# One chain for all sixteen causal heads, with the next head's logits ahead of the value product

## The chip, the cores and the metric

The kernel runs on one core of one Trainium2 chip. The metric is device microseconds (us) of one execution, and the median of several runs is what counts. The engines are TensorE (PE, with its weight loads PEld), VectorE (DVE), ScalarE (ACT), GpSimd (POOL) and SyncE (SP), whose queue issues the transfers.

## The reference

Two layers, each a SwiGLU half step, a mixing block and a second SwiGLU half step, on 512 tokens of width 1024. The mixing block has three branches on the same normalised input. Cut to the two causal branches:

```python
def block(args):                      # stick-breaking: 8 heads of 64
    z = q k^T * scale
    mask = key_pos < q_pos
    log_beta = log_sigmoid(z)
    log_not = where(mask, log_beta - z, 0)
    log_between = cumsum(log_not, reverse) - log_not
    w = where(mask, exp(log_beta + log_between), 0)
    return w @ v

def block(args):                      # forgetting: 8 heads of 64
    z = q k^T * scale + c_q - c_k     # c = cumsum(log_sigmoid(f))
    p = softmax(where(key_pos <= q_pos, z, min))
    return p @ v
...
merged = g_sb * (o_sb @ w_br_sb) + g_fx * (o_fx @ w_br_fox) + g_mem * (o_mem @ w_br_mem)
h = h + rmsnorm(merged @ w_out)       # g_* = sigmoid(u @ w_gate + b_gate)
```

The third branch is attention over 256 memory rows with four heads of 128.

## The kernel before

Every float32 matrix is kept as a high part and a low part, and a product is three matmuls (lines 210 to 212, `mm3`), each over 512 columns as a rule. The weights come as float32 from HBM in units of 512 KB (`raw_...`, a ring of two buffers), are split by ACT (high part, `wh_...`) and DVE (low part, `wl_...`) into rings of four, and are consumed once. On PE the matmuls therefore stand close behind each other almost everywhere, as long as weights and PSUM banks are there.

The order on PE is written by a planner at build time, `Queue`. It holds a list of jobs: the projections of q, k and v (`pq`, `pk`, `pv`), the gates (`pg`: input by `w_gate`, then a sigmoid) and the branch products (`pb`: attention output by `w_br`, times the gate). Beside the jobs runs a *chain*, a generator of the attention heads. `weave` goes on with the chain when its due time is reached, and fills the time until then with jobs, each counted by its columns (`PE_US`). A chain yields `("pe", t)` for work of its own on PE and `("wait", t)` for the time of other work that it asks for before its next stage. Jobs past a `limit` may not be taken yet; if no job is left, the planner's clock only jumps, and the next stage of the chain stands right behind the last on PE. `Q.past(n, t, limit)` runs the jobs up to number n and then up to `t` us of the job after it. A scheduler still places instructions of ACT, DVE and POOL among each other; the matmuls of a value product are pinned.

A causal head has four stages with three waits between them:

- Logits (`zs` for stick-breaking, line 1198; `zf` for forgetting, lines 1241 to 1252) and what ACT and DVE make of them: sigmoids and a product scan (lines 1204 to 1211), or maximum, exponential and division (1254 to 1258). Then a wait of `W_SB0` or `W_FX0`.
- The weights, float32, are taken apart into planes of 16 bits by ACT (`turn_out`, line 1137) and transposed by three transfers on SP's queue (`turn_over`, line 1146). Then `W_SB1` or `W_FX1`.
- The planes are joined again (`joined`, line 1156, by ACT for `pws`, by DVE for `pwf`) and split into high and low parts `pts`, `ptf` (lines 180 and 181). Then `W_SB2` or `W_FX2`.
- The value product (`attend`, line 1170, eight matmuls into `pvs` or `pvf`), and the head's output o (lines 1173 to 1175).

Before, the eight stick-breaking heads are woven one by one: a head's logits stand behind the value product of the head before. The eight forgetting heads are already one chain, `foxes`, in which the next head's logits are issued where a head asks for its last wait, `W_FX2`. Head names are layerless pairs: `1_0` is pair 1, head 0; the forgetting pairs go in the order 2, 3, 0, 1, so `1_1` is the last head of a layer.

Gates are computed in two ways (`sigmoid_neg`, lines 196 to 206): while `direct` is set, during the stick-breaking heads, by one ACT instruction (line 199); afterwards, with ACT's exponential and logarithm table, by four of ACT and one of DVE (lines 202 to 206). `forget_cumsum` (lines 1338 to 1349) needs the exponential and logarithm in the middle of the stick-breaking heads and changes tables there and back. The gate's PSUM bank comes free with DVE's instruction of line 205 or ACT's of line 199. There are four banks for jobs and value products together (`mm`) and four for logits (`z`).

Of the kernel before, what the change touches and what calls it, by code (L numbers as in the profile page):

```python
# [23 lines left out]
def kernel(  # L24
# [46 lines left out]
    NP = 4  # L71
# [30 lines left out]
    def stile(shape, tag, name, dt=F32R):  # L102
        return sb.tile(shape, dt, tag=tag, bufs=BUFS[tag], name=name)

    def blk(tag, name):
        return stile([P, 2, S], tag, name)
# [86 lines left out]
    def functions(name):  # L193
        tc.keep_in_program_order(nc.scalar.preload_act_table_set(name))
# [273 lines left out]
    Q = Queue()  # L468
# [710 lines left out]
    def cuts(name):  # L1179

        t = stile([P, CUT], "rs", "cut" + name, F32)
        nc.gpsimd.memset(t[:], 0.0)
        for c, before in ((CUT - 2 * P, 1), (CUT - P, 0)):
            o = t[:, c - before:c + P]
            nc.gpsimd.affine_select(out=o, in_=o, pattern=[[-1, P + before]], compare_op=ALU.not_equal, fill=1.0,
                                    base=before - 1, channel_multiplier=1)
        return t

    def stick_head(q, k, vts, pj, j, cut, ot, name):

        groups = []
        for rows in ((3,), (2,), (1, 0)):
            pz = pbank("z", f"z{name}_{rows[0]}")
            w0 = (rows[0] + 1) * P
            for i in rows:
                o = pz[:, (rows[0] - i) * 2 * P:][:, :max((i + 1) * P, 2 * P)]
                for kk in (j, 2 + j):
                    nc.tensor.matmul(o, q[:, j, i * P:(i + 1) * P], k[:, kk, :o.shape[1]], start=(i == rows[0] and kk == j),
                                     stop=(kk == 2 + j), skip_group_check=True)
            w = w0 + (len(rows) - 1) * P  # L1200
            zr, t, n = pz[:, :w], tmp(f"t{name}_{rows[0]}"), tmp(f"n{name}_{rows[0]}")

            nc.gpsimd.memset(t[:, w - 1:w], 0.0)
            nc.scalar.activation(n[:, :w], zr, AF.Sigmoid, scale=-1.0)
            nc.scalar.activation(t[:, :w - 1], zr[:, :w - 1], AF.Sigmoid)
            if len(rows) > 1:
                nc.vector.memset(n[:, w0:w0 + 1], 0.0)
            c1 = CUT if len(rows) > 1 else CUT - P
            back, one = n[:, 1:w][:, ::-1], cut[:, c1 - w:c1 - 1][:, ::-1]
            nc.vector.tensor_tensor_scan(back, back, one, 0.0, ALU.mult, ALU.add)  # L1210
            nc.vector.tensor_tensor(t[:, :w - 1], t[:, :w - 1], n[:, 1:w], ALU.mult)
            groups.append((rows, w, t, n))
        yield ("pe", 1.4)
        yield ("wait", W_SB0)
        for _, w, t, n in groups:
            turn_out(t, w, n)
            turn_over(n, w, t)
        yield ("wait", W_SB1)
        tri = joined([(rows, w, t) for rows, w, t, _ in groups], nc.scalar.copy, name)
        yield ("wait", W_SB2)  # L1220
        attend(pbank("mm", "pv" + name), j, vts, pj, tri, ot, name)
        yield ("pe", 1.2)

    def fox_pre(q, k, j, hd, cs, name):

        r, ro, _ = HEAD_ROWS[j]
        rs_ = slice(ro.start, min(ro.stop, 104))
        qk = stile([P, 2, S], "rs", "qk" + name)
        nc.gpsimd.tensor_copy(qk[r, 0], q[r, j])
        nc.gpsimd.tensor_copy(qk[r, 1], k[r, 2])  # L1230
        nc.gpsimd.memset(qk[ro, 0].bitcast(F32), 1.0)
        nc.vector.tensor_scalar(qk[rs_, 1], cs[rs_].bitcast(F32), sel[rs_, hd:hd + 1], None, ALU.mult)
        return qk
# [84 lines left out]
        split(ot[:, 0], ot[:, 1], pv[:])  # L1318
        yield ("pe", 1.3)

    W_SB0, W_SB1, W_SB2 = 7.0, 7.0, 5.0
    W_FX0, W_FX1, W_FX2 = 2.0, 6.3, 5.0
    W_MM0, W_MM1 = 6.0, 6.0
    W_K = 4.0

    FOX = (2, 3, 0, 1)
# [28 lines left out]
    def mixing(l, src, ks, vs, rest, dst):  # L1355
# [5 lines left out]
        st, marks = {}, {}  # L1361
# [138 lines left out]
        heads, fox = [(0, p) for p in range(NP)] + [(1, p) for p in FOX], []  # L1500
# [20 lines left out]
        limits = [marks["before", *h] for h in heads[2:]] + 3 * [marks["gates", 1]]  # L1521
        limits = [[min(n, marks["gates", 0]) if i < NP else n for n in limits[i:i + 2]] for i in range(len(heads))]
# [10 lines left out]
        def run():  # L1533
            Q.until(marks["first"])
            for i in range(NT):
                nc.sync.dma_start(hsave[i], hT[i][:])
            st["o", 2] = [blk("o", f"om{l}_{i}") for i in range(NMH)]

            def mems():
                def head(i):  # L1540
                    Q.until(marks["qm", i // 2])
                    return mem_head(st["qm"][i], ks, vs, i, st["o", 2][i], f"m{l}_{i}",
                                    lambda: Q.until(marks["values"]))


                def part(g):
                    for kind, us_ in g:
                        yield (kind, us_)
                        if kind == "wait":
                            return  # L1550
                gen = head(0)
                yield from part(gen)
                for i in range(NMH):
                    if i + 1 < NMH:
                        following = head(i + 1)
                        yield from ((k_, u_) for k_, u_ in part(following) if k_ == "pe")
                    for kind, us_ in gen:
                        if kind == "wait" and i + 1 == NMH:

                            Q.past(marks[0, 0], W_K, marks[0, 1])  # L1560
                            functions("sigmoid_and_others")
                            st["direct"] = True
                            begun[0, 0] = stick(0, 0)
                            yield next(begun[0, 0])
                        yield kind, us_
                    gen = following

            def stick(p, j):
                return stick_head(st["q", 0, p], st["k", 0, p], st["v", 0, p // 2], p % 2, j, st["cut"], st["o", 0][p],
                                  f"s{l}_{p}_{j}")  # L1570

            def pre(at, j):

                if j == 2:
                    at, j = at + 1, 0
                p = FOX[at] if at < NP else None
                if (p, j) not in fx and ("k", 1, p) in st:
                    fx[p, j] = fox_pre(st["q", 1, p], st["k", 1, p], j, 2 * p + j, st["cs"], f"{l}_{p}_{j}")

            def fox(at, j):  # L1580
                pre(at, j)
                p = FOX[at]
                return fox_head(st["q", 1, p], st["k", 1, p], st["v", 1, p // 2], p % 2, j, fx[p, j], st["o", 1][p],
                                f"f{l}_{p}_{j}", lambda: pre(at, j + 1))

            begun, fx = {}, {}
            st["cut"] = cuts(f"{l}")
            st["o", 0] = [blk("o", f"o{l}_0_{p}") for p in range(NP)]
            Q.weave(mems(), marks[0, 1])
            for p in range(NP):  # L1590
                Q.past(marks[0, p], W_K, limits[p][0])
                for j in range(2):
                    Q.weave(begun.pop((p, j), None) or stick(p, j), limits[p][j])
            functions("natural_log_exp_and_others")
            st["direct"] = False
            st["o", 1] = [blk("o", f"o{l}_1_{p}") for p in range(NP)]
            order = [(at, j) for at in range(NP) for j in range(2)]
            now = [0]

            def foxes():  # L1600

                def head(n):
                    at, j = order[n]
                    Q.past(marks[1, FOX[at]], W_K, limits[NP + at][0])
                    return fox(at, j)
                gen = head(0)
                for n in range(len(order)):
                    for kind, us_ in gen:
                        if us_ is W_FX2:
                            if n + 1 < len(order):  # L1610
                                following = head(n + 1)
                                yield next(following)
                            now[0] = min(n + 1, len(order) - 1)
                        yield kind, us_
                    gen = following

            def limit():
                at, j = order[now[0]]
                return limits[NP + at][j]
            Q.weave(foxes(), limit)  # L1620
            Q.until(limits[-1][-1])

        marks["run"] = run
# [110 lines left out]
    for l in LAYERS:  # L1734
        i, mn = 3 * l, []
# [43 lines left out]
```

## Time and profile before

| | |
|---|---|
| median of three runs | 2362.8 us (2358.9 to 2363.26) |
| the profiled execution | 2357.57 us, span from the first to the last instruction 2355.8 us |
| PE busy | 2310.8 us, 98% of the span |
| PEld, DVE, ACT | 1947.8 us (83%), 1795.6 us (76%), 1546.7 us (66%) |
| mean granted TensorE clock | 0.993 |
| layer 0: first stick-breaking logits to last forgetting value product | 434 to 782 us |
| layer 1: the same | 1602 to 1950 us |

Times in the views count from the span's start. A bracket behind an instruction is the idle time of its engine just before it, and what ended that idle time. Matmuls overlap: one over 512 columns is listed with 0.39 us, and the next starts 0.23 us after it.

### The profile page before, as it was taken

How to read it: one execution, taken by the hardware profiler on the slowest of the kernel's cores; microseconds unless marked ns; L12 is line 12 of the kernel's file. 1: busy time of each engine (PE TensorE's matmuls, PEld its weight loads, DVE VectorE, ACT ScalarE, POOL GpSimd, SP SyncE). 2: the span in 40 equal slices, each digit the busy share in tenths (PEclk: the TensorE clock that was granted, in tenths of full speed). 3: DMA queues.
4: the chain of work that ended last, by engine and by line, in shares of the span. 5: the costliest groups of instructions: out<-in, count | busy, mean ns of one | idle time of the engine just before them, and what ended most of it. 6: DMA issues, size and time to landing. Idle time of an engine off the chain costs nothing.

```text
span 2355.8 us, 30462 instructions
## 1 busy us (share of the span) xinstructions
PE 2310.8 (98%) x11303; PEld 1947.8 (83%) x11303; DVE 1795.6 (76%) x2285; ACT 1546.7 (66%) x2232; POOL 88.8 (4%) x182
## 2 busy tenths in 40 slices
PE   9999999999999899999999999999999989999998
PEld 8888888988887698888898888888888867888887
DVE  8877876656787688878798787765667876888785
ACT  6676565677778456774656765646787784567744
POOL 0000000001111000000000000000001200000000
PEclk9999999999999999999999999999999999999999
DMA  6667454354544655674646655533355455566744
GB/s 206 198 179 214 145 198 131 83 128 99 132 114 117 206 188 160 196 189 156 229 143 188 204 164 193 180 107 103 104 123 127 101 150 188 170 184 181 221 137 143
DMA packets 382841, 375.93 MB, mean 160 GB/s; under 512 B 163274, under 2 KB 274146, under 8 KB 382692
## 3 DMA queue, kind: packets, MB, share of 16 engines
q1 hardware_dynamic: 382596, 373.95, 54.3%
q8 instruction: 89, 1.46, 0.3%
q14 instruction: 60, 0.49, 0.1%
q0 software_dynamic: 96, 0.03, 0.0%
HBM read 319.39 MB, written 16.78 MB: 143 GB/s over the span
## 4 chain that ended last, share of the span: by engine, by line
PE 82%; DVE 6%; DMA 5%; ACT 5%; issue 2%; DVEq 0%; SPq 0%; ACTq 0%
PE pda L211 3%; PE pda L210 3%; PE pda L212 3%; PE pg L210 2%; PE pg L211 2%; PE pg L212 2%; PE pdc L211 2%; PE pdc L212 2%; PE pdc L210 2%; DMA pf<-nf 2%; PE pb L210 2%; PE pb L211 2%; PE pb L212 1%; PE pwc0g L210 1%; PE pwc1g L211 1%
## 5 line engine op out<-in xcount | busy, mean ns | idle before, releaser
L210 PE MATMUL pg<-us_a,wh_wg 128*128 128x512 f32 x384 | 150.1, 391 | 1.3 <-DVE k L181 1.3
L211 PE MATMUL pg<-us_a,wh_wg 128*128 128x512 f32 x384 | 149.6, 389 | 0.0
L212 PE MATMUL pg<-us_a,wl_wg 128*128 128x512 f32 x384 | 149.5, 389 | 0.0
L181 DVE TENSOR_TENSOR wl_da<-raw_da,wh_da 128x1024 fp32r<-128x1024 f32 x50 | 60.8, 1223 | 45.9 <-ACT wh_da L180 45.9
L181 DVE TENSOR_TENSOR wl_dc<-raw_dc,wh_dc 128x1024 fp32r<-128x1024 f32 x50 | 61.0, 1223 | 43.4 <-ACT wh_dc L180 43.4
L211 PE MATMUL pdc<-wl_dc,ahc 128*128 128x512 f32 x224 | 87.6, 391 | 0.0
L211 PE MATMUL pda<-wl_da,aha 128*128 128x512 f32 x224 | 87.6, 391 | 0.0
L212 PE MATMUL pda<-wh_da,ala 128*128 128x512 f32 x224 | 87.2, 389 | 0.0
L212 PE MATMUL pdc<-wh_dc,alc 128*128 128x512 f32 x224 | 87.2, 389 | 0.0
L210 PE MATMUL pdc<-wh_dc,ahc 128*128 128x512 f32 x224 | 86.5, 389 | 0.0
L210 PE MATMUL pda<-wh_da,aha 128*128 128x512 f32 x224 | 86.5, 389 | 0.0
L210 PEld LDWEIGHTS pg<-us_a,wh_wg 128*128 128x128 f32 x384 | 72.4, 188 | 16.7 <-PE pb L212 2.0
L212 PEld LDWEIGHTS pg<-us_a,wl_wg 128*128 128x128 f32 x384 | 72.1, 188 | 15.3
L211 PEld LDWEIGHTS pg<-us_a,wh_wg 128*128 128x128 f32 x384 | 72.3, 188 | 14.6
L180 ACT CAST wh_dc<-raw_dc 128x1024 fp32r<-128x1024 f32 x50 | 52.3, 1050 | 47.5 <-DMA raw_dc<-in_ffn_w_down_dram 16.1
L180 ACT CAST wh_da<-raw_da 128x1024 fp32r<-128x1024 f32 x50 | 52.1, 1049 | 46.8 <-PE pda L212 14.1
L184 DVE SCALAR_TENSOR_TENSOR wl_wg<-raw_wg,wh_wg 128x1024 fp32r<-128x1024 f32 x48 | 59.3, 1239 | 29.6 <-ACT wh_wg L183 29.3
L180 ACT CAST wh_uc<-raw_uc 128x1024 fp32r<-128x1024 f32 x44 | 46.4, 1054 | 38.0 <-PE pwc1g L212 9.2
L180 ACT CAST wh_ua<-raw_ua 128x1024 fp32r<-128x1024 f32 x44 | 46.2, 1053 | 32.9 <-PE pwa1g L212 9.3
L181 DVE TENSOR_TENSOR wl_uc<-raw_uc,wh_uc 128x1024 fp32r<-128x1024 f32 x44 | 53.7, 1220 | 16.7 <-ACT wh_uc L180 16.7
L183 ACT ACTIVATE wh_wg<-raw_wg 128x1024 fp32r<-128x1024 f32 x48 | 50.6, 1058 | 19.3 <-PE pv L1123 7.7
L181 DVE TENSOR_TENSOR wl_ga<-raw_ga,wh_ga 128x1024 fp32r<-128x1024 f32 x40 | 48.4, 1219 | 18.7 <-ACT wh_ga L180 18.7
(643 smaller groups left out, 7984.8 us busy)
## 6 DMA issues: line engine op xcount, KB each, us to landing
raw_da<-in_ffn_w_down_dram SPq DMA_DIRECT2D x66, 512.0 KB, 4.9
raw_dc<-in_ffn_w_down_dram SPq DMA_DIRECT2D x66, 512.0 KB, 4.6
raw_ga<-in_ffn_w_gate_dram SPq DMA_DIRECT2D x52, 512.0 KB, 4.7
raw_ua<-in_ffn_w_up_dram SPq DMA_DIRECT2D x52, 512.0 KB, 4.5
raw_gc<-in_ffn_w_gate_dram SPq DMA_DIRECT2D x52, 512.0 KB, 4.2
raw_uc<-in_ffn_w_up_dram SPq DMA_DIRECT2D x52, 512.0 KB, 4.4
raw_wg<-in_w_gate_dram SPq DMA_DIRECT2D x48, 512.0 KB, 3.5
raw_wo<-in_w_out_dram SPq DMA_DIRECT2D x24, 512.0 KB, 3.8
```

What stands on the lines that cost most here:

```text
L180: both = [nc.scalar.copy(h_ap, src)]
L181: make = lambda: nc.vector.tensor_tensor(l_ap, src, h_ap.bitcast(F32), ALU.subtract)
L183: both = [nc.scalar.activation(h_ap, src, AF.Copy, scale=scale)]
L184: make = lambda: nc.vector.scalar_tensor_tensor(l_ap, src, scale, h_ap.bitcast(F32), ALU.mult, ALU.subtract)
L210: nc.tensor.matmul(pt, lh, rh, start=start, stop=False, skip_group_check=free)
L211: nc.tensor.matmul(pt, lh, rl, start=False, stop=False, skip_group_check=free)
L212: nc.tensor.matmul(pt, ll, rh, start=False, stop=stop, skip_group_check=free)
```

## The change

The sixteen causal heads of a layer, eight stick-breaking and then eight forgetting, become one chain, `causal`. In all of them the next head's first stage, its logits, is issued where a head has joined its planes and asks for its last wait. The first forgetting head's logits so stand ahead of the last stick-breaking head's value product, and the change of ACT's tables to exponential and logarithm, with `direct` cleared, comes with them. The waits are set anew: the sum of a stick-breaking head's three goes from 19.0 to 16.1, that of a forgetting head from 13.3 to 13.2. `Q.past` is called only ahead of the first head of a pair, and the limit on jobs is that of the head whose logits were issued last.

```diff
-    W_SB0, W_SB1, W_SB2 = 7.0, 7.0, 5.0
-    W_FX0, W_FX1, W_FX2 = 2.0, 6.3, 5.0
+    W_SB0, W_SB1, W_SB2 = 5.0, 6.0, 5.1
+    W_FX0, W_FX1, W_FX2 = 2.0, 6.0, 5.2
...
-            Q.weave(mems(), marks[0, 1])
-            for p in range(NP):
-                Q.past(marks[0, p], W_K, limits[p][0])
-                for j in range(2):
-                    Q.weave(begun.pop((p, j), None) or stick(p, j), limits[p][j])
-            functions("natural_log_exp_and_others")
-            st["direct"] = False
-            st["o", 1] = [blk("o", f"o{l}_1_{p}") for p in range(NP)]
-            order = [(at, j) for at in range(NP) for j in range(2)]
+            order = [(br, i, j) for br in range(2) for i in range(NP) for j in range(2)]
             now = [0]
...
+            def head(n):
+                br, i, j = order[n]
+                if (br, i, j) == (1, 0, 0):
+                    functions("natural_log_exp_and_others")
+                    st["direct"] = False
+                    st["o", 1] = [blk("o", f"o{l}_1_{p}") for p in range(NP)]
+                if j == 0 and n:
+                    Q.past(marks[heads[br * NP + i]], W_K, limit())
+                return (fox if br else stick)(i, j)
...
+            def causal(gen):
                 for n in range(len(order)):
                     for kind, us_ in gen:
-                        if us_ is W_FX2:
+                        if kind == "wait" and us_ in (W_SB2, W_FX2):
                             if n + 1 < len(order):
                                 following = head(n + 1)
                                 yield next(following)
-                            now[0] = min(n + 1, len(order) - 1)
+                                now[0] = n + 1
                         yield kind, us_
                     gen = following
...
+            Q.weave(mems(), marks[0, 1])
+            Q.weave(causal(begun[0, 0]), limit)
             Q.until(limits[-1][-1])
```

The numbers of matmuls, vector instructions and transfers stay what they were, but for the gates: 28 instead of 22 take the longer way in the two layers together (18 more ACT instructions, 6 of DVE), and ACT's table loads go from 17 to 21.

How the program's order moves is shown at three places. First PE in layer 0, between the stick-breaking heads 1_0 and 1_1; `pvs_1_0` is the value product of the first, `zs_1_1` are the logits of the second, and L210 to L212 are matmuls of jobs. Before:

```order
L212 MATMUL pg_1_1_4519<-us_a_0_2946,wl_wg_1_0_0_4261 128x512
L1170 MATMUL pvs_1_0_4526<-pts_1_0_4493,v_0_0_1_3771 128x256 x4
L1170 MATMUL pvs_1_0_4526<-pts_1_0_4493,v_0_0_0_3695 128x384 x2
L1170 MATMUL pvs_1_0_4526<-pts_1_0_4493,v_0_0_0_3695 128x512 x2
L1198 MATMUL zs_1_1_3_4540<-k_0_1_3924,q_0_1_3882 128x512 x2
L1198 MATMUL zs_1_1_2_4550<-k_0_1_3924,q_0_1_3882 128x384 x2
L1198 MATMUL zs_1_1_1_4560<-k_0_1_3924,q_0_1_3882 128x256 x4
L210 MATMUL pg_1_1_4519<-us_a_0_2946,wh_wg_1_0_0_4260 128x512
```

And now:

```order
L212 MATMUL pg_2_3_4421<-us_a_0_2946,wl_wg_2_1_0_4089 128x512
L1198 MATMUL zs_1_1_3_4439<-k_0_1_3924,q_0_1_3882 128x512 x2
L1198 MATMUL zs_1_1_2_4449<-k_0_1_3924,q_0_1_3882 128x384 x2
L1198 MATMUL zs_1_1_1_4459<-k_0_1_3924,q_0_1_3882 128x256 x4
L210 MATMUL pg_2_3_4421<-us_a_0_2946,wh_wg_2_1_0_4088 128x512
...
L212 MATMUL pb_2_3_4492<-om_1_3329,wl_wb_2_1_0_4101 128x512
L1170 MATMUL pvs_1_0_4499<-pts_1_0_4434,v_0_0_1_3771 128x256 x4
L1170 MATMUL pvs_1_0_4499<-pts_1_0_4434,v_0_0_0_3695 128x384 x2
L1170 MATMUL pvs_1_0_4499<-pts_1_0_4434,v_0_0_0_3695 128x512 x2
L210 MATMUL pb_2_3_4492<-om_2_3330,wh_wb_2_1_0_4100 128x512
```

The logits have moved ahead of the value product, with 24 matmuls of jobs in between; from this value product to the next there are 90 matmuls of jobs before and 78 now (54 up to the next logits, 24 behind them).

Second, PE in layer 0 at the last two forgetting heads, 1_0 and 1_1, whose value products are `pvf_1_0` and `pvf_1_1`. Before:

```order
L212 MATMUL pg_1_6_6887<-us_a_1_2947,wl_wg_1_3_4_6546 128x512
L1170 MATMUL pvf_1_0_6912<-ptf_1_0_6824,v_1_0_1_5807 128x256 x4
L1170 MATMUL pvf_1_0_6912<-ptf_1_0_6824,v_1_0_0_5705 128x384 x2
L1170 MATMUL pvf_1_0_6912<-ptf_1_0_6824,v_1_0_0_5705 128x512 x2
L210 MATMUL pg_1_7_6933<-us_a_0_2946,wh_wg_1_3_0_6539 128x512
...
L212 MATMUL pg_1_7_6933<-us_a_1_2947,wl_wg_1_3_4_6546 128x512
L1170 MATMUL pvf_1_1_6985<-ptf_1_1_6980,v_1_0_1_5807 128x256
L210 MATMUL pb_1_0_7027<-o_1_0_5577,wh_wb_1_0_0_6721 128x512
```

And now:

```order
L212 MATMUL pb_0_7_6796<-o_0_1_3341,wl_wb_0_3_0_6410 128x512
L1170 MATMUL pvf_1_0_6803<-ptf_1_0_6725,v_1_0_1_5925 128x256 x4
L1170 MATMUL pvf_1_0_6803<-ptf_1_0_6725,v_1_0_0_5845 128x384 x2
L1170 MATMUL pvf_1_0_6803<-ptf_1_0_6725,v_1_0_0_5845 128x512 x2
L210 MATMUL pb_0_7_6796<-o_0_2_3342,wh_wb_0_3_0_6409 128x512
...
L212 MATMUL pg_1_6_6933<-us_a_1_2947,wl_wg_1_3_4_6650 128x512
L1170 MATMUL pvf_1_1_6949<-ptf_1_1_6897,v_1_0_1_5925 128x256 x4
L1170 MATMUL pvf_1_1_6949<-ptf_1_1_6897,v_1_0_0_5845 128x384 x2
L1170 MATMUL pvf_1_1_6949<-ptf_1_1_6897,v_1_0_0_5845 128x512 x2
```

Between the two value products stood 24 matmuls of jobs, all that was left (the gate `pg_1_7`); now there are 69, and half of gate `pg_1_6` and all of `pg_1_7` still follow. The logits of 1_1 stand 24 matmuls of jobs ahead of `pvf_1_0` before, and 27 now. Layer 1 moves in the same way.

Third, ACT in layer 0 at the cumulative sum of the forget gates (`fa`, `cs`), among the last stick-breaking heads; ACTIVATE of L1204 and L1205 are the sigmoids of a head's logits. Before:

```order
L180 CAST k_1_2_5102<-pk_1_2_5071 64x512
L1338 ACTIVATE fa_5114<-pfl_5109,bfor 8x512
L194 ACT_TABLE_LOAD
L180 CAST k_1_2_5102<-pk_1_2_5071 64x512
L1341 ACTIVATE fa_5114<-fa_5114 8x512
L180 CAST pts_2_1_5160<-pws_2_1_5154 128x896
L1342 ACTIVATE fa_5114<-fa_5114,one_t 8x512
L194 ACT_TABLE_LOAD
L1349 CAST cs_5123<-fb_5115 8x512
L199 ACTIVATE ga_2_6_5177<-pg_2_6_5141,bgate 128x512
```

And now:

```order
L1338 ACTIVATE fa_5178<-pfl_5173,bfor 8x512
L194 ACT_TABLE_LOAD
L180 CAST k_1_2_5166<-pk_1_2_5135 64x512
L1341 ACTIVATE fa_5178<-fa_5178 8x512
L1204 ACT_TABLE_LOAD
L1204 ACTIVATE ns_3_1_3_5233<-zs_3_1_3_5229 128x512
L1342 ACT_TABLE_LOAD
L1342 ACTIVATE fa_5178<-fa_5178,one_t 8x512
L194 ACT_TABLE_LOAD
L1349 CAST cs_5187<-fb_5179 8x512
L1205 ACTIVATE ts_3_1_3_5232<-zs_3_1_3_5229 128x511
L1204 ACTIVATE ns_3_1_2_5243<-zs_3_1_2_5239 128x384
```

A sigmoid of head 3_1, the last stick-breaking head, now falls between the exponential and the logarithm, so that ACT loads its tables four times there instead of twice, ahead of the rest of that head's sigmoids.

More of the change, by code (lines that the diff above doesn't have):

```diff
@@ L1588, in run, with limit @@
             st["o", 0] = [blk("o", f"o{l}_0_{p}") for p in range(NP)]
-            Q.weave(mems(), marks[0, 1])
-            for p in range(NP):
-                Q.past(marks[0, p], W_K, limits[p][0])
-                for j in range(2):
-                    Q.weave(begun.pop((p, j), None) or stick(p, j), limits[p][j])
-            functions("natural_log_exp_and_others")
-            st["direct"] = False
-            st["o", 1] = [blk("o", f"o{l}_1_{p}") for p in range(NP)]
-            order = [(at, j) for at in range(NP) for j in range(2)]
-            now = [0]
[L1600 to L1606, printed above, removed]
+            order = [(br, i, j) for br in range(2) for i in range(NP) for j in range(2)]
+            now = [0]
+            def head(n):
[7 more added lines that the diff above has]
+                return (fox if br else stick)(i, j)
+            def limit():
+                br, i, j = order[now[0]]
+                return limits[br * NP + i][j]
+            def causal(gen):
                 for n in range(len(order)):
                     for kind, us_ in gen:
-                        if us_ is W_FX2:
+                        if kind == "wait" and us_ in (W_SB2, W_FX2):
                             if n + 1 < len(order):
@@ L1612, in foxes @@
                                 yield next(following)
-                            now[0] = min(n + 1, len(order) - 1)
+                                now[0] = n + 1
                         yield kind, us_
                     gen = following
[L1617 to L1620, printed above, removed]
+            Q.weave(mems(), marks[0, 1])
+            Q.weave(causal(begun[0, 0]), limit)
             Q.until(limits[-1][-1])
```

## The prediction

> **What bounds the kernel now.** I read the page first, for the engine that is never free, then PE's waits, then the stretches in which they lie, then the order of time around the longest.
>
> ```profile
> PE 2310.8 (98%) x11303; PEld 1947.8 (83%) x11303; DVE 1795.6 (76%) x2285; ACT 1546.7 (66%) x2232; POOL 88.8 (4%) x182
> PE  9999999999999899999999999999999989999998
> ```
>
> PE is idle for 2355.8 − 2310.8 = 45.0 us in all. The change leaves PE's work as it is, so it can gain that idle time, and what a slower clock behind it costs, and no more. The waits of PE:
>
> ```profile
> PE pvf L1170 <- ACT ptf L180: 23.3, 2, 11.8
> PE pb L210 <- DVE ga L205: 3.9, 2, 2.0
> PE pvf L1170 <- DVE ptf L181: 1.9, 4, 0.6
> PE pvs L1170 <- DVE pts L181: 1.1, 2, 0.7
> PE pvs L1170 <- ACT pts L180: 0.8, 1, 0.8
> ```
>
> (us in total, times, longest.) More than half of the idle time is two waits of 11.6 and 11.8 us, one in each layer, in which a forgetting head's value product waits for its weights. The clock around the waits, layer 0 first, then layer 1:
>
> ```profile
> core 0: us, PE busy (x) PEld busy (x) DVE busy (x) ACT busy (x) POOL busy (x), PEclk, DMA share, GB/s
> 725.00:735.00 10.00, 8.39 (x30) 6.70 (x30) 7.83 (x16) 9.27 (x14) 0.00 (x0) 0.83 0.49 115
> 775.00:780.00 5.00, 1.39 (x4) 1.03 (x5) 2.55 (x5) 1.65 (x2) 0.00 (x0) 0.50 0.99 282
> 780.00:785.00 5.00, 5.00 (x20) 4.15 (x19) 1.88 (x3) 1.20 (x2) 0.00 (x0) 0.76 1.05 393
> 1895.00:1900.00 5.00, 5.00 (x16) 3.94 (x15) 3.27 (x6) 4.36 (x7) 0.00 (x0) 0.66 0.67 126
> 1945.00:1950.00 5.00, 3.63 (x11) 3.02 (x12) 3.07 (x5) 1.62 (x2) 0.00 (x0) 0.52 1.03 394
> ```
>
> Busy time at a granted clock c is (1 − c) lost. Behind the long wait that is 1.39 × 0.50 + 5.00 × 0.24 = 1.9 us in layer 0 and 3.63 × 0.48 = 1.7 us in layer 1. Behind the wait of 2.0 us for a gate (DVE's line 205) it is 8.39 × 0.17 = 1.4 and 5.00 × 0.34 = 1.7 us. So even a wait of 2.0 us costs about 3.5. The Trainium skill, "TensorE: Matmul & The Clock Gate", Part 1, gives the clock halved only after an idle window of about 3.4 us; the rows above show it lower after 2.0 us, and by the page such a wait would cost 2.0 instead of 3.5.
>
> Why the last head waits, in layer 0, in order of time:
>
> ```profile
> 753.30 0.48 PE L1251 MATMUL zf<-k,q 128*128 128x512 f32 x1
> 754.68 0.40 PE L210 MATMUL pg<-us_a,wh_wg 128*128 128x512 f32 x1
> 760.14 1.45 PE L1170 MATMUL pvf<-ptf,v 128*128 128x256 f32 x8
> 761.42 0.40 PE L210 MATMUL pg<-us_a,wh_wg 128*128 128x512 f32 x1
> 766.67 0.39 PE L212 MATMUL pg<-us_a,wl_wg 128*128 128x512 f32 x1
> 769.21 1.55 ACT L1137 COPY nf<-pf 128x768 uint16<-128x768 uint16 x2
> 770.91 3.16 SPq L1146 DMA_TRANSPOSE pf<-nf  x2
> 777.15 1.36 DVE L1156 COPY pwf<-pf 128x768 uint16<-128x768 uint16 x3 [3.09 <-DMA pf<-nf]
> 778.59 2.02 DVE L181 TENSOR_TENSOR ptf<-pwf,ptf 128x640 fp32r<-128x640 f32 x2
> 778.61 0.58 PE L1170 MATMUL pvf<-ptf,v 128*128 128x256 f32 x1 [11.55 <-ACT ptf L180]
> ```
>
> The head's logits begin at 753.3; ACT takes the last planes apart by 770.8, the transfers land by 777.2, the split ends at 780.6. That is 27.3 us from the logits to the last operand. PE had work for less: 24 matmuls from 754.68 to 760.14 (0.2275 us each), the value product of head 1_0, 24 more, and then nothing that the planner allowed. It ran out of jobs at 767.0.
>
> **The change part by part.**
>
> *Work moved to the end.* Each of the eight stick-breaking heads gives up 12 matmuls of jobs (90 to 78), 96 in a layer, or 96 × 0.2275 = 21.8 us, which now stand among the forgetting heads. Seven of those take 3 more each, and the last gets 69 instead of 24. From the last head's logits to its value product PE now has 1.4 (logits, 753.3 to 754.7) + 27 × 0.2275 = 6.1 + 1.3 (the value product at 760.14) + 69 × 0.2275 = 15.7, together 24.5 us. The head needed 25.3 us for its first matmul (778.61 − 753.30) and 27.3 for its last operand. Left at the unchanged speed of the head: 0.8 us, with perhaps 1 to 2 more inside the product. The ends for what is left in each layer: 0 if the head gets faster, since ACT now has less than one gate's work ahead of its planes instead of nearly two; 6 us if weight casts that ACT must do ahead of its planes hold it up as they did other heads. I take 1.0, nearest to the unchanged head. Such a short wait takes no clock. So 23.3 + 1.9 + 1.7 = 26.9 us come back, less 2 × 1.0: **24.9 us**.
>
> *The other waits for weights.* The stick-breaking heads now have more time from logits to value product:
>
> ```profile
> 488.23 1.44 PE L1198 MATMUL zs<-k,q 128*128 128x512 f32 x8
> 502.19 1.82 DVE L181 TENSOR_TENSOR pts<-pws,pts 128x640 fp32r<-128x640 f32 x2
> 509.92 1.45 PE L1170 MATMUL pvs<-pts,v 128*128 128x256 f32 x8
> ```
>
> The weights are ready at 504.0, 5.9 us ahead of need. From logits to value product it was 21.7 us; it becomes 1.3 + 24 × 0.2275 + 1.3 + 54 × 0.2275 + 1.3 + 24 × 0.2275 = 27.1 us. Asking for less other work does not eat this slack, it grows by 5.4 us. So the waits of `pvs` (1.1 + 0.8 us) go. A forgetting head in the middle gains 3 matmuls, 0.7 us, against waits of at most 0.6 (`pvf` for DVE, 1.9 in total), so most of those go too. I take **3.0** of the 3.8 us; ends 0 and 3.8.
>
> *ACT's load in the stick-breaking stage* hides all this, so I check the cover:
>
> ```profile
> 460.00:500.00 40.00, 40.00 (x230) 35.49 (x230) 24.87 (x33) 29.23 (x44) 2.56 (x6) 1.00 0.47 112
> 580.00:620.00 40.00, 38.48 (x179) 31.99 (x178) 29.17 (x36) 35.30 (x52) 5.35 (x14) 1.00 0.52 136
> ```
>
> Of 40 us ACT is busy for 29.2, 73%, so 16.8 us in a head's 23.0. A head now takes 78 × 0.2275 + 1.3 + 1.3 = 20.3 us. Even if all of ACT's 16.8 us stayed, that is 83%, and DVE's 24.9 of 40 become at most 71%. Both remain off the path; the 88% of the second row, at the forget gates' tables, cost PE 1.5 us there.
>
> *The table pile.* There ACT now loads tables twice more per layer:
>
> ```profile
> 577.44 0.67 ACT L1338 ACTIVATE fa<-pfl,bfor 8x512 f32<-8x512 f32 x1
> 578.13 1.28 ACT L194 ACT_TABLE_LOAD   x1
> 579.43 0.58 ACT L180 CAST k<-pk 64x512 fp32r<-64x512 f32 x1
> 582.13 1.28 ACT L194 ACT_TABLE_LOAD   x1
> ```
>
> That adds 2 × 1.28 = 2.6 us to ACT, and head 3_1's sigmoids queue behind the whole sum, about 5 us late by these rows. What is queued behind them: the sigmoid of gate 2_6, whose bank is wanted 9 us after the gate, and the last stick-breaking head, which has 11 us of slack by the count above. I take 0.5 us in each layer, **−1.0**; ends 0 and, with both loads fully on the path, −5.1. The Trainium skill, "ScalarE: Activation LUTs", on what a table load costs, puts a switch at 1.28 us and a drain of 1.38 us behind it, which speaks against this change. The row at 579.43 starts 0.02 us after the load, so no drain is seen here. By the page the extra would be 5.3 us a layer and the term perhaps −2.5.
>
> *More gates the long way.* Three more per layer, each three more ACT instructions and one of DVE. The forgetting stage grows with them by up to 21.8 us of PE's work, so their density rises little. What can show is the 2.0 us wait for a bank:
>
> ```profile
> 724.86 0.72 ACT L204 ACTIVATE ga<-ga,one_t 128x512 f32<-128x512 f32 x1
> 725.81 0.74 DVE L205 SCALAR_TENSOR_TENSOR ga<-pg,bgate,ga 128x512 f32<-128x512 f32 x1
> 726.61 0.50 PE L210 MATMUL pb<-o,wh_wb 128*128 128x512 f32 x1 [1.97 <-DVE ga L205]
> ```
>
> It struck the one gate that ended just as a head's logits began, so that its ACT work came behind the head's, and whose bank was wanted some 10 us later. In the new order again one gate per layer ends like that (0_2, with its bank wanted by the branch product 0_3 after 10 us). So I leave it: **0**; ends +7.0 (both go: 3.9 and clock 3.1) and −7.0 (twice as many).
>
> *At no cost:* the moved `Q.past` and limits change only which jobs stand where. The gates' way through DRAM and the next stage's weights were fetched during the long wait; their cover now is the 7 us of gate matmuls behind the last value product and eight branch products of 2.7 us each.
>
> *Sum:* 24.9 + 3.0 − 1.0 + 0 = 26.9 us against the profiled execution's 2357.6, so 2330.7. That execution lies 5.2 us below the median of the runs, 2362.8; against the median the sum gives **2336 us**.
>
> **The rivals.**
>
> *The last head gets slower with its new neighbours.* ACT's weight casts wait in its queue for PE to be done with older weights, and the planes stand behind them. If 6 us stay in each layer instead of 1, with 1.5 us of clock, the gain is 26.9 − 13.0 = 13.9 us, and the kernel runs 2349. Against it: the head's planes already came late before, 17 us after the logits, and now have less gate work ahead of them.
>
> *The forgetting stage becomes bound by ACT and DVE.* With two more bank waits of 3.5 us in each layer the gain shrinks by 14 to 13 us: 2350. (By the Trainium skill's rule on the clock, above, the same waits cost 8 and the time is 2344.) For it: between 725 and 735 us ACT is busy for 9.27 of 10 us and DVE for 7.83.
>
> *The stage behind starves.* If the transfers that used the long wait (282 to 393 GB/s there) now delay branch or output products by some 10 us per layer, the idle time only moves: about 2358, no change. Against it: the cover named above, 7 + 8 × 2.7 = 29 us.
>
> *Slower: the stick-breaking stage becomes bound by ACT's queue.* ACT takes its work in order, and sigmoids of one head now stand between planes of another. The sixteen stick-breaking heads of the two layers would have to wait for more than (26.9 + 4.7) / 16 = 2.0 us each to make the kernel slower by over 0.2%; at 2.5 us each it runs 2376. Against it: 83% at most, and 11 us of slack.
>
> **How the numbers follow.** My forecast has 0.70, the slower last head 0.12, the bound forgetting stage 0.09, the starved stage behind 0.05, the stick-breaking stage 0.04. The predicted time is the first's, 2336. The range goes down to 2322: all waits for weights and for gates gone (3.0 + 0.8 + 7.0 more), and a median nearer the lowest run shown. It goes up to 2351, which takes in the first two rivals. 0.2% (4.7 us) is about what a measurement of this kernel can tell from no change. Faster by more: 0.70 + 0.12 + 0.09 = 0.91; within it 0.05; slower 0.04.
>
> **What would show it.** In the profile after, the waits of `pvf` for ACT's `ptf` should be under 3 us in total, the granted clock 1.0 where the last forgetting head stands, the waits of `pvs` gone, PE's idle time some 22 us, and four table loads around head 3_1 with at most 1 us of wait behind them. I am wrong if PE still waits over 4 us for the last head, if new waits for `ga` appear several times per layer, or if `pvs` waits at every head.

## The result, and the profile after

The changed kernel takes 2346.0 us (median of four runs, 2345.4 to 2347.6), the kernel before 2362.7: a ratio of 0.9932, with a 95% interval of 0.9916 to 0.9948. That is 16.7 us faster. 2336 was forecast, in a range of 2322 to 2351.

From the page of the changed kernel, the engines and PE's slices:

```profile
PE 2315.8 (99%) x11303; PEld 1948.2 (83%) x11303; DVE 1803.4 (77%) x2291; ACT 1563.6 (67%) x2254; POOL 87.3 (4%) x182
PE   9999999999999999999999999999999999999998
```

Its waits of PE in the attention and the output projection (us in total, times, longest):

```profile
PE pvf L1170 <- DVE ptf L181: 9.0, 13, 1.4
PE pvf L1170 <- ACT ptf L180: 3.5, 2, 2.2
PE pwo L211 <- DVE wl_wo L181: 3.1, 4, 1.2
PE zf L1252 <- POOL qk L1230: 0.7, 1, 0.7
PE pvs L1170 <- DVE pts L181: 0.2, 1, 0.2
```

The two waits of 11.6 and 11.8 us are gone, and with them the two slices in the middle that read 8. The span is 2344.4 us, so PE is idle for 28.6 us (45.0 before; some 22 were forecast), and `pvf` waits 3.5 us for ACT's `ptf` (under 3 were forecast). The waits for a gate (`ga`) are gone too, which was not forecast. New are many short waits for `ptf`, and the output projection `pwo` waits for its weights. PE's timeline at the last forgetting head, layer 0 and then layer 1, and at the first, layer 0 and then layer 1:

```profile
765.36 0.80 PE L1170 MATMUL pvf<-ptf,v 128*128 128x256 f32 x4 [1.41 <-DVE ptf L181]
...
1925.91 0.80 PE L1170 MATMUL pvf<-ptf,v 128*128 128x256 f32 x4 [0.99 <-DVE ptf L181]
...
627.72 0.38 PE L1170 MATMUL pvf<-ptf,v 128*128 128x256 f32 x1 [1.36 <-ACT ptf L180]
628.99 0.79 PE L1170 MATMUL pvf<-ptf,v 128*128 128x256 f32 x4 [0.89 <-DVE ptf L181]
630.71 1.28 PE L1170 MATMUL pvf<-ptf,v 128*128 128x384 f32 x3 [0.93 <-DVE ptf L181]
...
1789.28 0.38 PE L1170 MATMUL pvf<-ptf,v 128*128 128x256 f32 x1 [2.16 <-ACT ptf L180]
```

The clock around them (windows of the changed kernel: busy time of PE, PEld, DVE, ACT, POOL, then the granted clock):

```profile
620.00:640.00 20.00, 16.82 (x68) 13.19 (x68) 15.42 (x28) 12.74 (x24) 3.94 (x6) 0.91 0.48 115
760.00:780.00 20.00, 18.39 (x81) 14.71 (x81) 11.97 (x16) 15.12 (x21) 0.00 (x0) 1.00 0.81 253
1790.00:1810.00 20.00, 18.52 (x74) 14.96 (x75) 15.39 (x28) 16.49 (x30) 4.18 (x7) 0.83 0.45 101
1920.00:1940.00 20.00, 18.80 (x85) 15.25 (x84) 12.07 (x15) 15.88 (x22) 0.00 (x0) 1.00 0.78 251
```

The last head (the second and fourth window) is close to the forecast: 1.4 + 0.2 and 1.0 + 0.2 us of wait, and no clock lost. The first forgetting head, 2_0, is new: 3.2 us of wait in layer 0 (1.36 + 0.89 + 0.93) and 4.0 in layer 1 (2.16 and the same two), and behind them a clock of 0.91 and 0.83, which is 16.82 × 0.09 + 18.52 × 0.17 = 4.7 us.

The two traces by stage, by the first starts of `zs`, of `pwo` and of `pgc` (the half step that follows) on PE in each layer:

| us, both layers | before | after | difference |
|---|---|---|---|
| mixing, first `zs` to first `pwo` | 369.5 + 369.6 | 359.6 + 359.9 | −19.6 |
| output projection, first `pwo` to first `pgc` | 45.3 + 46.6 | 47.3 + 50.7 | +6.1 |
| all else | 1524.7 | 1526.9 | +2.2 |
| span | 2355.8 | 2344.4 | −11.4 |

(Rounded to tenths.) Of the +2.2 us, 1.6 arise in the first 20 us, in code that is the same: PE's 150th matmul starts 1.6 us later there than in the kernel before. The window of the kernel before, and of the changed one:

```profile
0.00:20.00 20.00, 16.73 (x92) 12.00 (x93) 12.77 (x27) 14.28 (x26) 1.89 (x8) 0.91 0.87 293
```

```profile
0.00:20.00 20.00, 17.48 (x78) 11.48 (x79) 11.62 (x26) 13.30 (x24) 1.89 (x8) 1.00 0.80 272
```

PE starts 92 matmuls in the one and 78 in the other. The profiled executions of the kernels below start in the same way with 78 to 80 (six of them) or 87 to 92 (four), and e8, which is the kernel before but for its tables, is among the six. So it goes with the execution, not with the change. The profiled execution of before was 5 us under its median, that of after 0.2 us above; that makes the traces' 11.4 us the medians' 16.7.

### The profile page after: what moved, and what is told of

Read it like the earlier page. It is cut to its first block, busy times and chain, and to the rows that moved or that the text cites. A ratio compares the mean times of both kernels' runs of the same rounds, so it can differ in the third digit from the quotient of the medians.

```text
span 2344.4 us, 30464 instructions
## 1 busy us (share of the span) xinstructions
PE 2315.8 (99%) x11303; PEld 1948.2 (83%) x11303; DVE 1803.4 (77%) x2291; ACT 1563.6 (67%) x2254; POOL 87.3 (4%) x182
## 4 chain that ended last, share of the span: by engine, by line
PE 74%; DVE 9%; DMA 7%; ACT 7%; issue 3%; SPq 0%; DVEq 0%; ACTq 0%
PE pdc L211 3%; PE pdc L210 3%; PE pdc L212 3%; PE pda L211 2%; PE pda L210 2%; PE pda L212 2%; DMA pf<-nf 2%; PE pg L210 2%; PE pg L211 2%; PE pg L212 2%; PE pwc0g L211 1%; PE pwc1u L212 1%; PE pwc1g L212 1%; PE pwa1u L212 1%; PE pwa1g L212 1%
## 5 line engine op out<-in xcount | busy, mean ns | idle before, releaser
L210 PE MATMUL pg<-us_a,wh_wg 128*128 128x512 f32 x384 | 151.4, 394 | 0.0
L212 PE MATMUL pg<-us_a,wl_wg 128*128 128x512 f32 x384 | 150.8, 393 | 0.0
L212 PE MATMUL pdc<-wh_dc,alc 128*128 128x512 f32 x224 | 87.2, 389 | 0.0
L212 PE MATMUL pda<-wh_da,ala 128*128 128x512 f32 x224 | 87.2, 389 | 0.0
L210 PE MATMUL pda<-wh_da,aha 128*128 128x512 f32 x224 | 86.6, 390 | 0.2 <-ACT pda L893 0.2
L210 PE MATMUL pdc<-wh_dc,ahc 128*128 128x512 f32 x224 | 86.5, 389 | 0.0
L212 PEld LDWEIGHTS pg<-us_a,wl_wg 128*128 128x128 f32 x384 | 72.9, 190 | 15.6
L210 PEld LDWEIGHTS pg<-us_a,wh_wg 128*128 128x128 f32 x384 | 73.1, 190 | 15.2
L181 DVE TENSOR_TENSOR wl_uc<-raw_uc,wh_uc 128x1024 fp32r<-128x1024 f32 x44 | 53.7, 1221 | 16.1 <-ACT wh_uc L180 16.0
L1210 DVE TENSOR_TENSOR_SCAN ns<-ns,cut 128x383 f32<-128x383 f32 (+1 forms) x48 | 50.5, 1057 | 20.1 <-ACT ns L1204 19.9
L1156 ACT COPY pws<-ts 128x1024 uint16<-128x1024 uint16 (+1 forms) x64 | 56.5, 917 | 10.3 <-DMA ts<-ns 9.8
```

Source lines behind the costliest of these rows:

```text
L181: make = lambda: nc.vector.tensor_tensor(l_ap, src, h_ap.bitcast(F32), ALU.subtract)
L210: nc.tensor.matmul(pt, lh, rh, start=start, stop=False, skip_group_check=free)
L212: nc.tensor.matmul(pt, ll, rh, start=False, stop=stop, skip_group_check=free)
L1156: copy(block_words(word, i), over[:, :, c:c + i + 1])
```

## The experiments

Ten kernels ran, each against the kernel before on the same chip. "Mixing" and "projection" are the two stages of the table above, both layers summed, in the profiled execution.

| kernel | median us (range) | before | ratio, 95% interval | mixing | projection |
|---|---|---|---|---|---|
| changed | 2346.0 (2345.4–2347.6) | 2362.7 | 0.9932 [0.9916, 0.9948] | 719.5 | 98.0 |
| e1, two loads | 2342.7 (2340.3–2345.8) | 2361.3 | 0.9921 [0.9907, 0.9935] | 716.8 | 94.3 |
| e2, no tables | 2340.4 (2339.9–2340.7) | 2361.3 | 0.9911 [0.9897, 0.9924] | 712.0 | 96.5 |
| e3, old waits | 2365.6 (2363.6–2370.7) | 2361.3 | 1.0019 [1.0010, 1.0028] | 744.1 | 92.1 |
| e4, waits alone | 2348.5 (2347.7–2351.4) | 2361.3 | 0.9949 [0.9936, 0.9961] | 725.3 | 94.5 |
| e5, spread | 2343.6 (2338.7–2347.5) | 2361.3 | 0.9924 [0.9911, 0.9937] | 717.4 | 94.5 |
| e6, waits, no tables | 2349.8 (2345.6–2352.0) | 2361.3 | 0.9948 [0.9937, 0.9960] | 725.3 | 95.8 |
| e7, spread more | 2344.2 (2342.6–2346.2) | 2361.3 | 0.9927 [0.9914, 0.9940] | 722.7 | 91.3 |
| e8, before, no tables | 2357.9 (2355.6–2359.7) | 2361.3 | 0.9984 [0.9976, 0.9993] | 735.7 | 91.7 |
| e9, spread less | 2345.0 (2343.5–2346.7) | 2360.9 | 0.9931 [0.9918, 0.9943] | 720.9 | 95.8 |
| e10, spread in the middle | 2338.7 (2337.3–2340.3) | 2360.9 | 0.9906 [0.9891, 0.9921] | 708.6 | 99.1 |

**The order alone and the waits alone.** The change has two parts. e3 keeps the chain and sets the waits back:

```diff
-    W_SB0, W_SB1, W_SB2 = 5.0, 6.0, 5.1
-    W_FX0, W_FX1, W_FX2 = 2.0, 6.0, 5.2
+    W_SB0, W_SB1, W_SB2 = 7.0, 7.0, 5.0
+    W_FX0, W_FX1, W_FX2 = 2.0, 6.3, 5.0
```

> The one chain with logits ahead of the value product, and the waits as they were before (7.0, 7.0, 5.0 and 2.0, 6.3, 5.0). Jobs ahead of the last value product: 18 matmuls instead of 69. My theory, that the gain comes from the jobs moved to the end and not from the order of logits and value products: the long wait is back at 11 to 14 us in each layer, and with the late head 2_0 the kernel is no faster than before: 2360 to 2372 us. Rival, that the order gives the gain: 2340 to 2350.

The waits of PE in e3:

```profile
PE pvf L1170 <- ACT ptf L180: 21.4, 2, 11.6
PE pg L210 <- DVE sf L1174: 4.3, 2, 2.2
PE pb L210 <- ACT o L180: 4.2, 2, 2.5
```

The long waits are back (21.4 us), 2365.6 us. The chain alone gains nothing, it costs some 4 us (2 to 7 by the interval). e4 is the kernel before with the new waits and nothing else, the opposite of e3's edit:

> The kernel before with the new waits alone (5.0, 6.0, 5.1 and 2.0, 6.0, 5.2): stick-breaking heads still one by one, no crossing. 78 matmuls of jobs between the value products as in the change, 69 ahead of the last. My theory: weights were ready 5.9 us early in the kernel before, 2.7 us of that is given up, so pvs waits at most 1 to 4 us in a layer (at the tables), the last head under 2 us, and head 2_0 is not late: 2330 to 2340 us, faster than the change. Rival, that the logits must stand ahead for the shorter waits to be affordable: pvs waits 1 to 3 us at most heads, 16 to 48 us in all, 2350 to 2375.

It ran 2348.5, between the two: over what I expected, just under the rival's range, and without the rival's waits at most heads. The waits alone bring 12.8 us of the gain. What is missing against the changed kernel is one kind of wait, once in each layer:

```profile
PE pvs L1170 <- ACT pts L180: 9.9, 2, 5.3
PE pvf L1170 <- DVE ptf L181: 7.7, 10, 1.7
```

So the gain is work moved to the end by shorter waits, as forecast; the chain only covers a wait of 5 us that the shorter waits would open, worth some 4 us by the ratios (0.0017 × 2361; the intervals overlap) and 5.8 in mixing. I took this wait for the pile at the forget gates' tables, since it stands there.

**The tables.** In the changed kernel ACT's scheduler places a sigmoid of head 3_1 between the two halves of the forget gates' work, so that the tables are loaded four times (ACT's timeline, layer 0):

```profile
581.62 1.28 ACT L194 ACT_TABLE_LOAD   x1
582.91 0.58 ACT L180 CAST k<-pk 64x512 fp32r<-64x512 f32 x1
583.52 0.63 ACT L1341 ACTIVATE fa<-fa 8x512 f32<-8x512 f32 x1
584.17 1.28 ACT L1204 ACT_TABLE_LOAD   x1
585.47 0.60 ACT L1204 ACTIVATE ns<-zs 128x512 f32<-128x512 f32 x1
586.08 1.28 ACT L1342 ACT_TABLE_LOAD   x1
587.38 0.72 ACT L1342 ACTIVATE fa<-fa,one_t 8x512 f32<-8x512 f32 x1
588.12 1.28 ACT L194 ACT_TABLE_LOAD   x1
...
608.77 0.69 ACT L1256 ACTIVATE pf<-zf,stf 128x512 f32<-128x512 f32 x1 [0.46 <-DVE stf L1254]
```

The rest of that head's sigmoids follow at 589.9, its last casts end at 607, DVE's low parts of its weights stand ahead of the maxima (`stf`) of head 2_0, and only then comes the first exponential of head 2_0, 8.4 us behind its logits (PE, 600.35). Before it was 632.46 against 628.04, 4.4 us. e1 orders every sigmoid behind the switch back and every switch behind the sigmoids ahead of it, so that two loads a layer go; PE's order is the same:

```diff
     def functions(name):
+        ins = nc.scalar.preload_act_table_set(name)
+        tc.keep_in_program_order(ins)
+        for i in sigmoids:
+            tc.add_manual_dep(ins.ins, i.ins.name, NOSYNC, reason="tables")
...
+    def with_sigmoid(ins):
+        for i in switch:
+            tc.add_manual_dep(ins.ins, i.ins.name, NOSYNC, reason="tables")
```

> The changed kernel with two orders on ScalarE added, and nothing else: a head's sigmoids and the gates' stand behind the switch back to the sigmoid table after the forget gates, and a switch stands behind the sigmoids before it. ACT loads tables twice around head 3_1 instead of four times; PE's order is the same, row for row. My theory: the shortfall against the forecast is that pile of table loads, which makes the first forgetting head (2_0) late, 3.2 and 4.0 us of PE's waits and a lower clock behind them. Then 2.6 us less on ACT gives those waits 2 to 3 us shorter in each layer and most of the clock back: 2337 to 2341 us against 2346. Rival, that crossing from one kind of head to the other is late by itself: no change, 2345 to 2347, with pvf 2_0 still waiting over 2.5 us.

It ran 2342.7, less of a gain than I expected: by the ratios 0.0011 × 2361 = 2.6 us under the changed kernel, within what the intervals leave open, and 2.7 us less in mixing. The waits of `pvf` for ACT fell from 3.5 to 0.3 us, those for DVE rose to 10.8. At head 2_0 alone the waits fell from 7.2 to 2.7 us, but at the other forgetting heads they rose from 5.3 to 8.4, and in layer 0 the clock now fell at the last head (the same window as above):

```profile
760.00:780.00 20.00, 18.41 (x75) 14.70 (x74) 12.91 (x17) 14.74 (x21) 0.00 (x0) 0.91 0.73 256
```

So the extra loads do make head 2_0 late, as my theory had it, but most of what their absence saves there is lost again at the heads behind. e2 is e1 with the forget gates' exponential and logarithm replaced by copies, so that no table is loaded for them (the logarithm of the sigmoid is left out):

> As the last one, and the exponential and logarithm of the forget gates are replaced by two copies with a factor, so that no table is switched there at all (left out: the logarithm of the forget gates' sigmoid; as many instructions). The upper end of what the tables cost the changed kernel. My theory: no wait over 1 us at head 2_0, clock 1.0 there, 2333 to 2338 us. Rival: under 2 us below the run with two loads, pvf 2_0 still waiting.

It ran 2340.4, again above the range expected, with 7.5 us less in mixing than the changed kernel. PE still waited for `pvf`, now one head later:

```profile
PE pvf L1183 <- DVE ptf L181: 9.6, 13, 1.4
PE pwo L224 <- DVE wl_wo L181: 3.1, 4, 1.2
```

Does the change pay more for the tables than the kernel before? e8 takes them out of that:

> The kernel before with the forget gates' exponential and logarithm replaced by copies and no table loads for them (the logarithm of the sigmoid is left out). It prices the tables in the kernel before. My theory: they cost little there, since the waits of pvs were 1.9 us in all and the tables were loaded once per layer beside slack: 2358 to 2361, 0 to 3 us under the kernel before. Rival: the tables cost about as much there as in the changed kernel (5.6 us): 2354 to 2357; then the pile is no loss of the change.

2357.9, so they cost 3.4 us (interval 1.7 to 5.7) before, against 5.0 in the changed kernel (0.9932 − 0.9911). My figure was 0 to 3, the rival's 5.6; the interval leaves both open. By mixing it is 3.4 and 7.5. What the change adds at the tables is therefore 2 to 4 us by these figures, which is within the noise of the runs; the tables are not shown to be the main loss.

**What the chain covers.** e6 is e4 without the tables in the same way:

> The kernel before with the new waits alone (as e4), and the exponential and the logarithm of the forget gates replaced by copies, without their two table loads: the logarithm of the forget gates' sigmoid is left out. My theory: the chain's only gain over the waits alone is that it covers the pile at the tables (pvs waited for pts 9.9 us there, 2 times, and the clock fell behind it). Without the pile the chain has nothing to cover: no pvs wait over 1 us, 2337 to 2342, level with the chain without tables (2340.4). Rival: the chain also gives the stick-breaking heads time that they need elsewhere, as the prediction has it with 5.4 us more for each; then pvs waits move to other heads and the time is 2345 to 2349.

It ran 2349.8 and still waits for `pts` at the same place. My reading of e4 was wrong. Seen in e6's trace, PE and ACT, the head's logits, its sigmoids and its value product:

```profile
565.36 1.44 PE L1198 MATMUL zs<-k,q 128*128 128x512 f32 x8
...
569.55 1.06 ACT L183 ACTIVATE wh_wg<-raw_wg 128x1024 fp32r<-128x1024 f32 x1 [3.20 <-DMA raw_wg<-in_w_gate_dram]
571.28 0.60 ACT L1204 ACTIVATE ns<-zs 128x512 f32<-128x512 f32 x1
...
587.87 1.56 ACT L180 CAST pts<-pws 128x640 fp32r<-128x640 f32 x2
...
588.64 0.58 PE L1170 MATMUL pvs<-pts,v 128*128 128x256 f32 x1 [4.35 <-ACT pts L180]
```

ACT stood for 3.2 us in front of a weight cast whose transfer had not landed, and the sigmoids behind it in its queue began 5.9 us after the logits. Layer 1 and both layers of e4 show the same. In the changed kernel the logits of that head stand further ahead, and its sigmoids start 0.7 us behind them (559.68 and 560.35), ahead of that cast in ACT's queue. It is this delay of a stick-breaking head that the chain covers, with the 5.4 us more that it gives each of them from logits to value product. The tables have little part in it: without them the waits for `pts` are 8.7 us instead of 9.9, and the time is the same.

**The short waits of the forgetting heads.** e5 is e1 with time moved from the stick-breaking heads' waits to the forgetting heads':

```diff
-    W_SB0, W_SB1, W_SB2 = 5.0, 6.0, 5.1
-    W_FX0, W_FX1, W_FX2 = 2.0, 6.0, 5.2
+    W_SB0, W_SB1, W_SB2 = 5.0, 5.3, 4.6
+    W_FX0, W_FX1, W_FX2 = 2.0, 6.7, 5.7
```

> As e1 (the two pairs of table switches in each layer made one), and the planner's waits changed once more: stick-breaking 5.0, 5.3, 4.6 instead of 5.0, 6.0, 5.1, forgetting 2.0, 6.7, 5.7 instead of 2.0, 6.0, 5.2. By the order of PE's instructions each stick-breaking head gives up about 0.7 us of jobs, and each forgetting head gets 0.6 to 0.7 us more between its logits and its value product (3.2 us more at one), the last head 0.7. My theory: what is left of PE's waits in the forgetting stage (pvf for DVE, 10.8 us, 14 times, at most 1.4) is work that still stands in the wrong place, so these waits fall by about 8 us to 3, the clock loses nothing behind them, and the time is 2333 to 2338. Rival: a forgetting head's operands come as fast as ACT and DVE make them, and jobs that are added bring their own work for both, so each head gets later by what it was given: waits of 8 to 11 us, 2341 to 2346. Third: the stick-breaking heads have no slack left, and pvs waits for pts several times in a layer: 2345 and more.

The waits of `pvf` went, from 10.8 us to none in the list, but the time stayed (2343.6; the profiled execution is the fastest of six, 2338.7, so it does not show what the median's 5 us more are). In their place:

```profile
PE pb L223 <- DVE fb L1358: 6.2, 2, 3.1
PE zf L1264 <- POOL k L1431: 2.7, 2, 1.6
PE zf L1265 <- POOL qk L1243: 2.4, 2, 1.2
```

e7 goes further (4.4, 4.7, 4.1 and 2.3, 7.3, 6.4):

> As e5, further: stick-breaking 4.4, 4.7, 4.1, forgetting 2.3, 7.3, 6.4. Each stick-breaking head gives up 2.6 to 3 us of jobs against e1, forgetting heads get 2 us more. The work ahead of the forget gates' job now ends so late that the job falls behind the last sigmoids: 13 table loads in all instead of 17, with nothing left out of the computation. My theory: if the waits are misplaced work, this goes as far as e5 or further, pvf's waits under 2 us and none at the tables: 2329 to 2336. Against it: the forget gates' sums now come later, and the first forgetting head's logits may wait for them (up to 5 us in a layer), and the stick-breaking heads, with 0.7 + 2.6 us less, may wait for pts: 2340 to 2355. Rival as in e5, heads set by ACT and DVE: 2341 to 2346.

2344.2, with 7.5 us of `zf` for POOL's `k`, 3.7 us of `zs` for it and 0.7 us of `pvf`; the sooner a chain wants its head, the closer that head stands behind its own projection. e9 (5.0, 5.6, 4.8 and 2.0, 6.4, 5.5) and e10 (5.0, 5.3, 4.9 and 2.0, 6.6, 5.7) look for a setting with neither:

> As e1, with half the spread of e5: waits of stick-breaking heads 5.0, 5.6, 4.8, of forgetting heads 2.0, 6.4, 5.5. By PE's order a stick-breaking head gives up 0.6 us of jobs against e1; the jobs that the third pair's projections belong to stand later, so that its logits come 13.0 us behind the value product ahead of them instead of 9.1. In e5 the waits of pvf went, but the same time came back in waits for k and qk from POOL (5.1 us) and for the forget gates' DVE work (6.2 us). My theory: the jobs that a stick-breaking head gives up include projections that a later head needs, so a wait saved at a value product is paid at the logits or at the gates: pvf waits 3 to 7 us, the other two kinds 4 to 9 us, time 2340 to 2345, level with e1 and e5. Rival: between e1 and e5 there is a setting with neither: both kinds under 4 us each, time 2334 to 2339.

> As e5 but with the stick-breaking heads' last wait 4.9 instead of 4.6 and the forgetting heads' second 6.6 instead of 6.7: 5.0, 5.3, 4.9 and 2.0, 6.6, 5.7. By PE's order the third pair's logits come 11.0 us behind the value product ahead of them (e5 12.3, e1 9.1), while forgetting heads keep the 0.6 us more. My theory as for e9: what is saved at value products is paid at projections: 2340 to 2345, with waits for POOL's k and qk of 2 to 5 us. Rival: a setting with neither kind, 2334 to 2339.

e9 ran 2345.0, in the range of my theory, with one head a layer that waits 4.0 us for its `k` (7.9 in all); but `pvf` waits only 1.6 us in all, less than the 3 to 7 expected. In e10 the rival holds: 2338.7, and PE's waits behind the projections are these (e9's for `k`, then e10's in these stages):

```profile
PE zf L1264 <- POOL k L1431: 7.9, 2, 4.0
```

```profile
PE pwo L224 <- DVE wl_wo L181: 3.0, 4, 0.8
PE pb L223 <- DVE fb L1358: 2.2, 2, 1.3
PE pv L1134 <- DVE ga L1493: 1.9, 2, 1.0
PE pwo L223 <- ACT wh_wo L180: 1.6, 2, 0.8
...
PE zf L1265 <- POOL qk L1243: 1.2, 2, 0.8
```

No wait of `pvf` or `pvs` is left, and mixing takes 708.6 us: 10.9 less than in the changed kernel, 8.2 less than in e1, 30.5 less than before. The time beats both kernels: 0.9906, 22.1 us under the kernel before, about 6 under the changed one by the ratios (0.0026 × 2361; the intervals touch, the ranges of the runs, 2337.3 to 2340.3 and 2345.4 to 2347.6, do not). It is the best of four settings tried, and its interval overlaps those of the other three.

More time is not the whole reason why these waits went. Head 2_1 has fewer matmuls of jobs between its logits and its value product in e10 than in e1 (99 against 105; e9 has 96), but its last operand comes 26.2 us behind its logits in both layers of e10, where in e1 it came after 30.7 and 32.6. The other work around the heads has moved too. At head 2_0 of e10, layer 0, ACT casts `ptf` first and the projection's `q` later, where the changed kernel has them the other way round (its lines stand in the next section); whether this order is what made the heads faster was not tried apart:

```profile
618.01 0.73 ACT L180 CAST ptf<-pwf 128x640 fp32r<-128x640 f32 x1 [0.99 <-DVE pwf L1169]
622.64 0.59 ACT L183 ACTIVATE q<-pq 64x512 fp32r<-64x512 f32 x1
```

## Why the prediction was right, and where not

The direction, the main mechanism and the range held; the gain came out at 16.7 us instead of 26.9. That the range held is in part luck: without the 7.0 us at the gates, which were not forecast, the time would have been some 2353, outside it. By its terms, from the rows above:

- **Work moved to the end**, +24.9 us. The waits of the last head went from 23.3 us and 3.6 of clock to 2.8 us (1.41 + 0.21 + 0.99 + 0.20) and none: 24.1. I had left 1.0 us in each layer; it was 1.6 and 1.2. This term was right, and e3 and e4 show that the waits alone do it.
- **The table pile**, −1.0 us, is where the forecast went wrong, in size and by its place. I looked for the delay at head 3_1 and found 11 us of slack there, which was true (`pvs` waits 0.2 us in all). The forecast has no look at the head behind it, 2_0, whose logits now stand among 3_1's last work. Before, its last operand came 19.1 us behind its logits (628.04) in layer 0; now it comes 30.3 us behind them (600.35):

```profile
635.05 1.06 ACT L1137 COPY nf<-pf 128x1024 uint16<-128x1024 uint16 x1
...
646.11 1.07 DVE L181 TENSOR_TENSOR ptf<-pwf,ptf 128x896 fp32r<-128x896 f32 x1
```

```profile
617.43 1.04 ACT L1137 COPY nf<-pf 128x1024 uint16<-128x1024 uint16 x1
...
626.25 0.59 ACT L183 ACTIVATE q<-pq 64x512 fp32r<-64x512 f32 x1 [3.14 <-DVE q L184]
626.94 0.72 ACT L180 CAST ptf<-pwf 128x640 fp32r<-128x640 f32 x1
...
629.57 1.08 DVE L181 TENSOR_TENSOR ptf<-pwf,ptf 128x896 fp32r<-128x896 f32 x1
```

  (The kernel before, then the changed one.) Of these 11.2 us, 4.0 arise ahead of the first exponential, at the pile and 3_1's last weights. Another 6.1 arise between the exponential and the planes `nf` (8.7 us against 2.6), where ACT does a gate the long way, casts of weights and 3_1's output first; and at the end ACT stands 3.1 us in front of a cast of `q` that waits for DVE, with `ptf` behind it. The value product of 2_0 cost 7.16 us of waits and 4.66 of clock, 11.8 in all, instead of 1.0, far beyond my lower end of 5.1. So the tables alone are not the cause: without the extra loads 2_0 waits 2.7 us, but the time falls by only 2.6 (e1), without any tables the waits go to the next head (e2), and in e10 they go altogether though two loads a layer stay.
- **The other waits for weights**, +3.0 us. The part on stick-breaking heads held (1.9 to 0.2 us). The part on the middle forgetting heads did not: I had costed 0.7 us more work against waits of 0.6, as if the heads came no later. Apart from head 2_0 and the last, `pvf` waits 2.5 us now (1.9 before), so the term is +1.1. The added gates the long way lie in the same stage; whether they are what made the heads later was not tried apart.
- **Gates the long way**, 0 us with ends of ±7. Both waits for a bank went, and the clock loss behind them: 3.9 + 3.1 = +7.0, the upper end. I had one gate per layer waiting again; why none does was not tried.

These make 24.1 + 1.1 − 11.8 + 7.0 = 20.4 us. Outside the terms two waits of gates for `k`, 1.3 us in all, went, and one of `zf` for `qk`, 0.7 us, came. That makes 21.0, against 19.6 measured in mixing; 1.4 us are not assigned.

- **At no cost: the transfers and the stage behind.** This failed too. The output projection takes 6.1 us more. Of that 2.5 us are waits for its weights (3.1 + 0.4 against 1.0), 1.5 us clock (48.53 us busy at 0.97 in layer 1), the rest isn't assigned:

```profile
1971.00:2018.00 47.00, 45.99 (x212) 1.00 0.53 169
```

```profile
1957.00:2008.00 51.00, 48.53 (x213) 0.97 0.55 175
```

(Windows of PE alone over the output projection of layer 1, before and then after: busy time, matmuls, clock.) The rival of the starved stage behind so came in with 3 us a layer instead of 10, next to the forecast and not in its place. Among the kernels of the table this stage goes from 91.3 to 99.1 us, and it is longest in e10, whose mixing is shortest. Why its weights come later was not tried.

The other rivals: the stick-breaking stage bound by ACT did not happen. The forgetting stage bound by ACT and DVE is half true: its waits are for their `ptf`, but e10 shows that ACT and DVE have room, since PE waits nowhere for `ptf` there.

On the clock, the Trainium skill's page "TensorE: Matmul & The Clock Gate", Part 1, would have it kept through waits under about 3.4 us. At head 2_0 no single wait is over 2.16 us, and the clock is 0.83 over the window; the measurement decides.

## What to carry to other kernels

When a planner's waits are shortened, look for the next late operand not only at the head whose slack was counted but also at the one behind it in the queues of ACT and DVE, which work in order. Time given to one group of heads is taken from the jobs ahead of another, and those jobs hold that group's own projections; a setting is good where neither the value products nor the logits wait. A few tenths of a microsecond in the planner's waits change which of them waits (e5 against e10); the times of the two do not lie far enough apart to be told from noise by their intervals. When a long wait goes, count what the stage behind had been given by it, weights above all.

## What the runs showed of the hardware

- Short waits can lower the granted clock: one of 1.97 us went with 0.83 over 10 us (the kernel before), 1.36, 0.89 and 0.93 us within 4.4 us with 0.91 over 20 us, and 2.16, 0.89 and 0.93 us with 0.83. The lengths alone do not decide it: 1.41 and 0.21 us at the last head of the changed kernel went with 1.00, and 1.39 and 0.20 us at the same head of e1 with 0.91 over 20 us.
- The first 20 us of the same code hold 78 to 80 matmuls in some executions and 87 to 92 in others, and the first stick-breaking logits come at 435.6 to 436.7 us in the first kind and at 434.1 to 435.9 in the second. Two single profiles can differ by some 1.5 us for that alone.
- A table load takes 1.28 us, and an instruction of ACT that waits for nothing else starts 0.01 to 0.02 us after it, also with four of them within 8 us.
